# An encoder layer in fp32 halves: two gate products swapped, w_down's blocks in nine buffers, keys kept negated, and a split queued behind an addition

## The chip, the cores and the metric

The kernel runs on one core of a Trainium2 chip. The metric is the device time of one execution in microseconds; the time of a kernel is the median over its runs. The profile shows one execution of its own, taken by the hardware profiler. Engines are named as there: PE (matmul), PEld (its weight loader), DVE (vector engine), ACT (scalar engine), POOL (GpSimd), SP (the engine that issues most DMAs).

## The reference

One layer of a bidirectional encoder over 512 tokens of width 1024, all in float32, with 256 fixed memory tokens:

```python
memn = rms_norm(mem, mem_norm_g)
n = rms_norm(h, mix_norm_g)
proj = n @ w_in
gate_a, gate_b = sigmoid(proj[..., OFF_GA:OFF_GB]), sigmoid(proj[..., OFF_GB:])
ya = s5_branch(proj[..., :OFF_U], ...)          # state space, both directions
yb = sgu_branch(zu, zv, ...)                    # spatial gating in chunks of 128
h = h + (gate_a * (ya @ w_proj_a) + gate_b * (yb @ w_proj_b)) @ w_out
# memory cross-attention, 4 heads of 256
hn = rms_norm(h, xattn_norm_g)
q, k, v = hn @ w_q, memn @ w_k, memn @ w_v
s = einsum('blhd,bmhd->bhlm', q, k) * (256 ** -0.5)
h = h + einsum('bhlm,bmhd->blhd', softmax(s), v).reshape(...) @ w_xo
# SwiGLU, hidden width 2816
f = rms_norm(h, ffn_norm_g)
h = h + (silu(f @ w_gate) * (f @ w_up)) @ w_down
out = rms_norm(h, final_norm_g)
```

## The kernel before

**Precision.** Every matmul operand x is kept as two rounded halves, hi and lo, with x = hi + lo. `split` makes them: ACT casts x to hi (line 85), DVE subtracts hi from x to give lo (line 86). A product is three matmuls, hi·hi, hi·lo and lo·hi (`mm3`).

**Weights.** Weight blocks of 512 KB are loaded from DRAM by SP's queue into buffers tagged "raw" (three of them in the pool `wp`), split into "hi" and "lo" (three buffers each), and used by PE. A list `plan` holds one entry per block, in the order of use: a key, its loads with a number of entries by which each is asked for ahead, and a function `make` that splits the block. `next_w` hands out the blocks in that order: when entry i is used, it asks for the loads that are due (`LOADS` = 3 entries ahead unless the entry says otherwise) and for the splits of entries up to i + 2 (`SPLITS`).

**Seven products in place of eight.** Several large products (the gates of the second branch, the queries, gate and up projections, w_down) are done as 2 x 2 blocks with seven block products instead of eight, numbered 1, 5, 2, 6, 3, 7, 4. They need sums of weight blocks and of token blocks. For w_down, the sums of weights are made in DRAM: an SP copy into `dsum` (line 311), then a POOL DMA that adds the other block onto it (line 312), placed along the plan by `plan_sums`. The sums of tokens are made by DVE in place in `make_tokens`.

**Gates.** The two halves of the second gate (i = 0, 1) are interleaved by `ORDER`, whose entries are (product, half). Products 1, 6, 7 and 4 of a half accumulate in one bank gx[i], 5 and 3 in gq[i], 1 (copied) and 2 in gv[i]. After product 7, `kept` copies gx to SBUF on ACT (line 1250) and `minus` subtracts it from gq on DVE (line 1254). The weight of product 4 is made in place from product 6's: a DVE subtraction and then a POOL DMA that adds a block onto it (line 256).

**Attention.** `k_evac` splits the keys from PSUM into kt_hi and kt_lo. `scores` computes, for each head and each pair of token tiles, psc = q·k; then a row maximum `mx` (line 1528), its scaled negative `nm` (line 1529), two exponentials with `nm` as bias that also sum up (line 1531), a reciprocal and two scalings (line 1535). `turn_probs` transposes the probabilities on PE (line 1545).

**FFN.** `plan_units` and `plan_unit` make the gate and up projections in ten units; their blocks sit in "raw" and in two buffers each of the tags "b21", "t" and "b22" of a pool `stp[0]` that stays open to the end of the kernel. w_down follows: seven products of six blocks each (CHUNKS), from `plan_down`, the first two of them set between the last unit's products. For each product `make_tokens` splits the tokens for two blocks at a time (tag "s" in the profile). Results are added onto h by `onto_h` (line 1876), tile by tile. Near the end, products 7 and 4 use the same two banks dx[0] and dx[1] one after the other; `row_by_row` does two blocks for token tile 0 first and then for token tile 1.

**Order of the work.** Matmuls and other instructions are given in program order, but the order in each engine's queue is laid down ahead of time by a list scheduler that goes by priorities and its own costs (`schedule_with_timeline_sim=True`); on the chip each engine then works through its queue in that order, waiting on semaphores. `tc.issue_after(x)` puts the instructions traced in its block behind x, for those of them that run on x's engine; `keep_in_program_order` keeps one in its place.

Of the kernel before, what the change touches and what calls it, by code (L numbers as in the profile page):

```python
# [17 lines left out]
P = 128  # L18
# [34 lines left out]
def hybrid_layer_kernel(  # L53
# [29 lines left out]
    def split(dst_hi, dst_lo, src):  # L83

        hi = nc.scalar.copy(dst_hi, src)  # L85
        lo = nc.vector.tensor_tensor(dst_lo, src, dst_hi.bitcast(F32), ALU.subtract)  # L86
        if pinned[0]:
            in_order(hi)
            in_order(lo)
        return hi, lo  # L90
# [131 lines left out]
            plan.append(((w_q, 512 * n, q), [(LOADS, load)], lambda got=got: halves(got.pop("raw"))))  # L222

    GATES = [(w_in, OFF_GB), (w_in, OFF_GB + 512)]
    ORDER = ((1, 0), (1, 1), (2, 0), (2, 1), (5, 0), (6, 0), (5, 1), (7, 0), (6, 1), (3, 0), (7, 1), (4, 0), (4, 1), (3, 1))
    gate_place = [None]

    def plan_gates():
# [83 lines left out]
            plan[j + step][1].append((0, lambda d=dst, x=more: nc.gpsimd.dma_start(d, x, accum_op=ALU.add)))  # L312

    def plan_down(w, make_tokens, entries):
        for q in DOWN:
            for c in range(CHUNKS):
                got = {}

                def load(q=q, c=c, got=got):
                    src = down_block(*DSRC[q], c) if q in DSRC else down_sum(q, c)  # L320
                    got["raw"] = wp.tile([P, 2, 512], F32, tag="raw", name="wraw", bufs=3)[:, :src.shape[1]]
                    nc.sync.dma_start(got["raw"], src)

                def make(q=q, c=c, got=got):
                    make_tokens(q, c)
                    return halves(got.pop("raw"))

                entries.append(((w, q, c), [(LOADS, load)], make))

    plan_tok(w_in, OFF_V, KD)  # L330
    for c0 in range(0, SW, 256):
# [1128 lines left out]
    kt_lo = ap_.tile([P, KD, M], F32R, name="kt_lo")  # L1460
    vts = []

    def k_evac(m, j, ps):
        split(kt_hi[:, m, :], kt_lo[:, m, :], ps)

    def v_evac(half):
        def f(t, ps):
# [44 lines left out]

    def scores(hd, behind=None):
        q_hi, q_lo = qs.pop(hd)
        scale = XD ** -0.5
        prob = ap_.tile([P, NT, M], F32, tag="prob", name="prob", bufs=1) if hd % 2 == 0 else \
            np_.tile([P, NT, M], F32, tag="gain", name="prob", bufs=2)
        for i in range(2):
            ps = bank("psc").rearrange("p (t m) -> p t m", t=2)
            for tt in range(2):  # L1520
                t = 2 * i + tt
                tsl = slice(t * P, (t + 1) * P)
                for k in range(2):
                    with nullcontext() if behind is None else tc.issue_after(behind):
                        mm3(ps[:, tt, :], (q_hi[:, k, tsl], q_lo[:, k, tsl]),
                            (kt_hi[:, 2 * hd + k, :], kt_lo[:, 2 * hd + k, :]), k == 0, k == 1)
            mx, nm, sm, rs = (ap_.tile([P, 2], F32, tag=k, name=k, bufs=4) for k in ("mx", "nm", "sm", "rs"))
            nc.vector.tensor_reduce(mx, ps, AX.X, ALU.max)
            nc.vector.tensor_scalar(nm, mx, -scale, None, ALU.mult)
            for tt in range(2):  # L1530
                nc.scalar.activation(prob[:, 2 * i + tt, :], ps[:, tt, :], AF.Exp, bias=nm[:, tt:tt + 1],
                                     scale=scale, accum_out=sm[:, tt:tt + 1])
            nc.vector.reciprocal(rs, sm)
            for tt in range(2):
                nc.vector.tensor_scalar(prob[:, 2 * i + tt, :], prob[:, 2 * i + tt, :], rs[:, tt:tt + 1], None, ALU.mult)
        return prob
# [201 lines left out]

    made, last_job = {}, []

    def token_pieces(f, ts, c):
        if c < 2:
# [3 lines left out]
    def make_tokens(q, c):  # L1748

        if c % 2 or (q, c // 2) in made or (q, c) == (1, 0) and not last_job:  # L1750
            return
        c //= 2
        hi, lo = made[q, c] = sums_place((1, 2, 4)[len(made) % 3], 4, 256)
        f, ts = {1: (0, T0), 5: (0, T1), 6: (0, T1), 2: (1, T0), 7: (0, T0), 3: (1, T0), 4: (1, T1)}[q]
        for src, ks in token_pieces(f, ts, c):
            split(hi[:, ks], lo[:, ks], src)
        a, b_, c_, d_ = (token_pieces(f_, ts_, c) for ts_ in (T0, T1) for f_ in (0, 1))
        for (q11, _), (q12, _), (s21, _), (q22, _) in zip(a, b_, c_, d_):
            if q == 5:
                V.tensor_tensor(s21, s21, q11, ALU.subtract)  # L1760
            elif q == 3:
                V.scalar_tensor_tensor(q11, s21, -1.0, q22, ALU.mult, ALU.subtract)
            elif q == 2:
                V.tensor_tensor(q12, q12, s21, ALU.add)
# [108 lines left out]
    def onto_h(ps, t0, half, op):  # L1873
        for t in range(2):
            hs = h[:, t0 + t, HALF[half]]
            nc.vector.tensor_tensor(hs, hs, ps[t], op)  # L1876

    def row_by_row(q, c0):

# [21 lines left out]
        finish(t)  # L1901
    down_product(dx, 7, False, range(CHUNKS - 2))
    row_by_row(7, CHUNKS - 2)
    onto_h(dx, 2, 0, ALU.subtract)
    for t in range(2, 4):
        first_half(t, 0)

    held = []
    row_by_row(4, 0)
    for c in range(2, CHUNKS):  # L1910
        ops_ = next_w(w_down, 4, c)
        if c < CHUNKS - 2:
            rows_product(dx, 4, c, ops_, (0, 1), slice(0, 512), False, c == CHUNKS - 3)
        else:
            held.append((c, ops_))
# [46 lines left out]
```

## Time and profile before

| | |
|---|---|
| median of three runs | 869.28 us (869.12 to 870.82) |
| the profiled execution | 870.48 us, span 868.7 us |
| granted TensorE clock | 0.996 |
| busy PE, PEld, DVE, ACT, POOL | 855.1, 760.1, 648.3, 474.8, 106.0 us |
| instructions | 14845 |
| HBM read, written | 148.70 MB, 37.20 MB |

The span runs from the first to the last instruction of the program; the execution's own time has what lies around it. Times in rows of the trace are counted from the start of the span. The kernel's stages lie roughly so: gates from 262 to 303 us, attention's scores from 457 to 487, the units from 543 to 760, w_down from there to the end. In a row of the timeline stand start, duration, engine, line, operation, out<-in, shapes and count, and in brackets how long the engine had been idle and what released it.

### The profile page before, as it was taken

To read this page: it belongs to the slowest core of one execution; us is meant where nothing else is said; L and a number is where in the kernel's file an instruction comes from. 1 tells how busy PE (TensorE), PEld (TensorE's weight loads), DVE (VectorE), ACT (ScalarE), POOL (GpSimd) and SP (SyncE) were. 2 spreads that over 40 slices of the span, in tenths; PEclk is the share of its full clock that TensorE was granted. 3 is DMA by queue.
4 is the path that set the end of the run, shared out by engine and by line. 5 is a ranking of instruction groups with operands and counts; after the bars stand their busy time and mean duration, and the time that the engine had idled before them with its cause. 6 is when DMAs were issued, how large, how long until landed. Compare 5 with 4: busy or idle time off the path is not lost.

```text
span 868.7 us, 14845 instructions
## 1 busy us (share of the span) xinstructions
PE 855.1 (98%) x5894; PEld 760.1 (88%) x5894; DVE 648.3 (75%) x897; ACT 474.8 (55%) x704; POOL 106.0 (12%) x157
## 2 busy tenths in 40 slices
PE   8999999999999999999999999999999999999996
PEld 6788888888789988899899888999999999987875
DVE  5699589968748668679658646767877778898875
ACT  5544875276437534467457444655545454655664
POOL 1001155100601000110010001001111111000000
PEclk9999999999999999999999999999999999999999
DMA  7549279745639586944687143557798786476572
GB/s 247 163 115 265 66 216 242 160 128 169 158 92 252 138 230 206 274 124 160 217 257 214 53 151 103 146 146 178 166 240 230 183 222 143 134 213 216 201 246 94
DMA packets 110119, 155.40 MB, mean 179 GB/s; under 512 B 8969, under 2 KB 77089, under 8 KB 109986
## 3 DMA queue, kind: packets, MB, share of 16 engines
q1 hardware_dynamic: 91746, 128.27, 44.9%
q0 software_dynamic: 18016, 25.66, 18.5%
q8 instruction: 46, 0.75, 0.3%
q10 hardware_dynamic: 288, 0.52, 0.2%
q14 instruction: 23, 0.19, 0.1%
HBM read 148.70 MB, written 37.20 MB: 214 GB/s over the span
## 4 chain that ended last, share of the span: by engine, by line
PE 91%; DMA 3%; ACT 2%; DVE 2%; issue 1%; SPq 0%; POOL 0%; POOLq 0%; ACTq 0%; DVEq 0%
PE pf L396 25%; PE pt L396 18%; PE px L1241 13%; PE dx L396 7%; PE pq L1241 6%; PE pv L1241 3%; PE gx L1241 3%; PE qx L1241 3%; PE dq L396 2%; PE gq L1241 1%; PE psc L396 1%; PE po L396 1%; PE qq L1241 1%; PE py L1034 1%; PE ptr L563 1%
## 5 line engine op out<-in xcount | busy, mean ns | idle before, releaser
L85 ACT CAST whi<-wraw 128x1024 fp32r<-128x1024 f32 (+1 forms) x133 | 136.9, 1029 | 143.1 <-PE pf L396 42.1
L86 DVE TENSOR_TENSOR wlo<-wraw,whi 128x1024 fp32r<-128x1024 f32 (+1 forms) x133 | 158.5, 1192 | 71.9 <-ACT whi L85 70.9
L396 PE MATMUL pf<-xn,whi 128*128 128x512 f32 x320 | 99.8, 392 | 0.0
L1241 PE MATMUL px<-fn,whi 128*128 128x256 f32 x480 | 83.2, 276 | 0.0
L1241 PEld LDWEIGHTS px<-fn,whi 128*128 128x128 f32 x480 | 72.5, 188 | 0.2
L396 PEld LDWEIGHTS pf<-xn,whi 128*128 128x128 f32 x320 | 59.6, 188 | 12.5 <-issue 0.5
L85 ACT CAST whi<-b 128x1024 fp32r<-128x1024 f32 x40 | 42.2, 1054 | 51.4 <-PE px L1241 26.5
L86 DVE TENSOR_TENSOR wlo<-b,whi 128x1024 fp32r<-128x1024 f32 x40 | 48.9, 1222 | 28.5 <-ACT whi L85 28.5
L1241 PE MATMUL px<-fn,wlo 128*128 128x256 f32 x240 | 66.4, 277 | 0.0
L396 PE MATMUL pf<-xn,wlo 128*128 128x512 f32 x160 | 62.9, 393 | 0.0
L1241 PE MATMUL pq<-s,whi 128*128 128x256 f32 x320 | 55.0, 276 | 0.0
L396 PE MATMUL dx<-whi,s 128*128 128x512 f32 x170 | 53.3, 391 | 0.4 <-DVE h L1876 0.4
L86 DVE TENSOR_TENSOR wlo<-t,whi 128x1024 fp32r<-128x1024 f32 x30 | 36.7, 1224 | 19.4 <-ACT whi L85 19.4
L85 ACT CAST whi<-t 128x1024 fp32r<-128x1024 f32 x30 | 31.6, 1054 | 35.3 <-PE pv L1241 12.6
L1241 PEld LDWEIGHTS pq<-s,whi 128*128 128x128 f32 x320 | 48.2, 188 | 0.0
L1241 PEld LDWEIGHTS px<-fn,wlo 128*128 128x128 f32 x240 | 45.1, 188 | 0.0
L1241 PE MATMUL pq<-s,wlo 128*128 128x256 f32 x160 | 44.2, 276 | 0.0
L396 PE MATMUL pt<-whi,xn 128*128 128x512 f32 x128 | 42.8, 407 | 0.3 <-ACT xn L85 0.2
L396 PEld LDWEIGHTS dx<-whi,s 128*128 128x128 f32 x170 | 31.8, 188 | 7.6 <-issue 0.8
L312 POOL DMA_DIRECT2D dsum<-in_w_down_dram x12 | 13.3, 1108 | 189.8 <-DMA dsum<-in_w_down_dram 189.8
L396 PEld LDWEIGHTS pf<-xn,wlo 128*128 128x128 f32 x160 | 30.1, 188 | 6.3 <-issue 0.2
L396 PE MATMUL dx<-wlo,s 128*128 128x512 f32 x85 | 32.9, 389 | 0.0
(480 smaller groups left out, 2329.5 us busy)
## 6 DMA issues: line engine op xcount, KB each, us to landing
wraw<-in_w_in_dram SPq DMA_DIRECT2D x35, 512.0 KB, 5.8
dsum<-in_w_down_dram SPq DMA_DIRECT2D x20, 512.0 KB, 5.9
wraw<-dsum SPq DMA_DIRECT2D x20, 512.0 KB, 3.7
b<-in_w_gate_dram SPq DMA_DIRECT2D x15, 512.0 KB, 4.3
b<-in_w_up_dram SPq DMA_DIRECT2D x15, 512.0 KB, 5.2
wraw<-in_w_down_dram SPq DMA_DIRECT2D x15, 512.0 KB, 4.8
dsum<-in_w_down_dram POOLq DMA_DIRECT2D x10, 512.0 KB, 7.5
dsum<-dsum POOLq DMA_DIRECT2D x10, 512.0 KB, 6.4
```

The lines of the kernel that those rows point to most:

```text
L85: hi = nc.scalar.copy(dst_hi, src)
L86: lo = nc.vector.tensor_tensor(dst_lo, src, dst_hi.bitcast(F32), ALU.subtract)
L312: plan[j + step][1].append((0, lambda d=dst, x=more: nc.gpsimd.dma_start(d, x, accum_op=ALU.add)))
L396: last_mm[0] = nc.tensor.matmul(ps, a[x], b[y], start=start and i == 0, stop=stop and i == 2, skip_group_check=free)
L563: tr = nc.tensor.transpose(ps[:, j, :], src[:, k * P:(k + 1) * P], ident)
L1034: in_order(nc.tensor.matmul(ps[64 * j:64 * j + 64, :], a, b, start=g % 4 == k == 0, stop=k == 2, tile_position=(0, 64 * j), skip_group_che ...
L1241: nc.tensor.matmul(ps[:, j, :], a[x], b[y], start=start and j == k == i == 0, stop=k == 3 and i == 2, skip_group_check=True)
```

## The change

Four places are edited.

1. `ORDER` has (4, 0) where (3, 0) stood, and the reverse, two places apart with (7, 1) between them.
2. `plan_down` gives its blocks buffers in a fixed turn: three "raw", and two each of "b21", "t" and "b22", nine in all; every block from the third on asks for its load six entries ahead rather than three. The first two blocks stay as they were.
3. `k_evac` stores the keys times -1/16 (a scaled activation on ACT and a multiply-subtract on DVE). So psc comes out as minus the scaled scores; a row minimum of it is directly the bias, the exponential runs with scale -1, and the instruction that scaled and negated the maximum is gone.
4. `onto_h` returns its first addition. That of product 7 is kept in `held_back` until product 4's first two blocks have been taken, and `make_tokens` traces its splits behind it meanwhile.

```diff
-    ORDER = ((1, 0), (1, 1), (2, 0), (2, 1), (5, 0), (6, 0), (5, 1), (7, 0), (6, 1), (3, 0), (7, 1), (4, 0), (4, 1), (3, 1))
+    ORDER = ((1, 0), (1, 1), (2, 0), (2, 1), (5, 0), (6, 0), (5, 1), (7, 0), (6, 1), (4, 0), (7, 1), (3, 0), (4, 1), (3, 1))
...
     def plan_down(w, make_tokens, entries):
+        turns = ("raw", "b21", "raw", "t", "b22", "raw", "b21", "t", "b22")
...
-                def load(q=q, c=c, got=got):
+                def load(q=q, c=c, got=got, n=len(entries)):
                     src = down_block(*DSRC[q], c) if q in DSRC else down_sum(q, c)
-                    got["raw"] = wp.tile([P, 2, 512], F32, tag="raw", name="wraw", bufs=3)[:, :src.shape[1]]
+                    tag = turns[n % len(turns)] if n > 1 else "raw"
+                    got["raw"] = (wp if tag == "raw" else stp[0]).tile(
+                        [P, 2, 512], F32, tag=tag, name="wraw", bufs=3 if tag == "raw" else 2)[:, :src.shape[1]]
                     nc.sync.dma_start(got["raw"], src)
...
-                entries.append(((w, q, c), [(LOADS, load)], make))
+                entries.append(((w, q, c), [(LOADS if len(entries) < 2 else 6, load)], make))
...
+    scale = XD ** -0.5
+
     def k_evac(m, j, ps):
-        split(kt_hi[:, m, :], kt_lo[:, m, :], ps)
+        nc.scalar.activation(kt_hi[:, m, :], ps, AF.Copy, scale=-scale)
+        nc.vector.scalar_tensor_tensor(kt_lo[:, m, :], ps, -scale, kt_hi[:, m, :].bitcast(F32), ALU.mult, ALU.subtract)
...
-        scale = XD ** -0.5
...
-            mx, nm, sm, rs = (ap_.tile([P, 2], F32, tag=k, name=k, bufs=4) for k in ("mx", "nm", "sm", "rs"))
-            nc.vector.tensor_reduce(mx, ps, AX.X, ALU.max)
-            nc.vector.tensor_scalar(nm, mx, -scale, None, ALU.mult)
+            nm, sm, rs = (ap_.tile([P, 2], F32, tag=k, name=k, bufs=4) for k in ("nm", "sm", "rs"))
+            nc.vector.tensor_reduce(nm, ps, AX.X, ALU.min)
             for tt in range(2):
                 nc.scalar.activation(prob[:, 2 * i + tt, :], ps[:, tt, :], AF.Exp, bias=nm[:, tt:tt + 1],
-                                     scale=scale, accum_out=sm[:, tt:tt + 1])
+                                     scale=-1.0, accum_out=sm[:, tt:tt + 1])
...
-    made, last_job = {}, []
+    made, last_job, held_back = {}, [], [None]
...
         for src, ks in token_pieces(f, ts, c):
-            split(hi[:, ks], lo[:, ks], src)
+            with nullcontext() if held_back[0] is None else tc.issue_after(held_back[0]):
+                split(hi[:, ks], lo[:, ks], src)
...
     def onto_h(ps, t0, half, op):
         for t in range(2):
             hs = h[:, t0 + t, HALF[half]]
-            nc.vector.tensor_tensor(hs, hs, ps[t], op)
+            added = nc.vector.tensor_tensor(hs, hs, ps[t], op)
+            first = added.ins if t == 0 else first
+        return first
...
-    onto_h(dx, 2, 0, ALU.subtract)
+    held_back[0] = onto_h(dx, 2, 0, ALU.subtract)
     for t in range(2, 4):
         first_half(t, 0)

     held = []
     row_by_row(4, 0)
+    held_back[0] = None
```

## The prediction

> **What bounds the kernel now.** I read the page first (engine totals), then the waits of PE, then the timeline around each wait that lies behind the first changed line, because a change here is worth only what PE stops waiting for.
>
> ```profile
> PE 855.1 (98%) x5894; PEld 760.1 (88%) x5894; DVE 648.3 (75%) x897; ACT 474.8 (55%) x704; POOL 106.0 (12%) x157
> ...
> PE ppt L1545 <- DVE prob L1535: 1.1, 1, 1.1
> ...
> PE dv L396 <- DVE wlo L86: 0.5, 1, 0.5
> ...
> PE dx L396 <- DVE h L1876: 0.4, 1, 0.4
> PE gq L1241 <- DVE u L1254: 0.4, 1, 0.4
> ...
> PE dv L396 <- ACT whi L85: 0.3, 1, 0.3
> ```
>
> PE is busy 98% of the span, so the bound is TensorE's stream of matmuls, and the change neither adds nor removes a matmul. What can be won is idle time of PE. The five waits shown are those that stand behind the gates; they add to 2.7 us, and each edit of the change touches one of them. But the idle column understates a stall: a matmul's drawn end overlaps its successor. I therefore price each stall by start times: the step over the gap, less the ordinary step.
>
> **Edit 1, gate products.** PE and DVE at the third product on gq, then ACT and POOL before it:
>
> ```profile
> 288.11 0.28 PE L1241 MATMUL gx<-gse,wlo 128*128 128x256 f32 x1
> 288.80 0.39 PE L1241 MATMUL gq<-gsd,whi 128*128 128x256 f32 x1 [0.41 <-DVE u L1254]
> 289.02 0.28 PE L1241 MATMUL gq<-gse,whi 128*128 128x256 f32 x1
> 289.14 0.28 PE L1241 MATMUL gq<-gsd,wlo 128*128 128x256 f32 x1
> 288.06 0.68 DVE L1254 TENSOR_TENSOR u<-gq,u 128x512 f32<-128x512 f32 x1
> 282.75 1.05 ACT L85 CAST whi<-wraw 128x1024 fp32r<-128x1024 f32 x1 [0.96 <-ACT u L1341]
> 286.79 0.58 ACT L1250 COPY u<-gx 128x512 f32<-128x512 f32 x1
> 276.50 1.35 POOL L256 DMA_DIRECT2D gw<-in_w_in_dram  x1 [1.82 <-issue]
> DMA to landing us min/median/max: 4.5/6.1/6.7
> ```
>
> The ordinary step of a 256-column matmul is 0.11-0.12 (289.02 to 289.14). The step over the gap is 0.69, and the next is 0.22 instead of 0.11: the stall costs 0.58 + 0.11 = 0.69. Product (3,0) accumulates into gq[0], which `minus` of product (7,0) still reads until 288.74, with one product in between. With (4,0) in its place PE writes gx[0], whose last reader is the copy that ends at 287.37, before PE gets there at about 288.2; (3,0), two products later, finds gq[0] long free. What moves with (4,0): its split goes into the slot where (3,0)'s ran, at 282.75, and it must find the POOL accumulation landed, issued at 276.50, so about 282.6 by the median and 283.2 by the maximum. That is a tie with 282.75, but behind it cast (1.05) and subtraction need some 2.3, and PE arrives at 288.2: 2.6 us of cover even at the maximum. The tiles' ring of "ev" buffers and the raw buffers keep their counts; (3,0)'s raw buffer is freed two products (2 x 24 matmuls of 0.113, 5.4) later, so w_glu's second block is fetched that much later on SP, and it is used five products and one block after that. Bounds: gain 0 (the tie goes wrong) to 0.69; the value is 0.69, since the cover is wide.
>
> **Edit 2, keys kept negated, one instruction less per pair of tiles.** DVE, then PE:
>
> ```profile
> 474.10 0.68 DVE L1528 TENSOR_REDUCE mx<-psc 128x2 f32<-128x512 f32 x1
> ...
> 476.43 0.16 DVE L1529 TENSOR_SCALAR nm<-mx 128x2 f32<-128x2 f32 x1
> ...
> 478.90 0.15 DVE L1533 RECIPROCAL rs<-sm 128x2 f32<-128x2 f32 x1
> 479.34 0.69 DVE L1528 TENSOR_REDUCE mx<-psc 128x2 f32<-128x512 f32 x1 [0.28 <-PE psc L396]
> ...
> 480.01 0.61 DVE L1535 TENSOR_SCALAR prob<-prob,rs 128x256 f32<-128x256 f32 x2
> 479.02 0.28 PE L396 MATMUL psc<-kt_hi,qq 128*128 128x256 f32 x1
> 480.41 0.70 PE L1545 MATMUL ppt<-ident,prob 128*128 128x128 f32 x4 [1.11 <-DVE prob L1535]
> L85 ACT CAST kt_hi<-pf x8: 363/373/381, 387.5 to 407.9; 128x256 fp32r<-128x256 f32 x8
> L1531 ACT ACTIVATE prob<-psc,nm x16: 462/473/495, 460.1 to 486.8; 128x256 f32<-128x256 f32 x16
> ```
>
> The stall is 480.41 - 479.02 - 0.11 = 1.28. Its cause is the order of DVE's queue: head 1's probabilities (480.01) stand behind a row reduction of head 2, which itself waits for PE until 479.34. They stand so late because the chain has four hops on DVE and ACT, and between hops DVE takes longer work: the reduction ended at 474.78, yet `nm` ran at 476.43. Without `nm` the exponentials can start right behind the reduction, up to 1.65 earlier; the reciprocal at 478.90 would then be possible near 477.3 and both scalings before PE asks at 479.1. Bounds: at the low end nothing but `nm`'s own slot goes (at most its 0.16), at the high end the whole 1.28; below zero only if the new order puts a second reduction in front, another 0.69. I take 1.28, as 1.65 is over it. The eight evacuations of keys become a scaled activation: the cast takes 0.373, an activation of the same shape from PSUM 0.473, so at most 8 x 0.10 = 0.8 of ACT in a stage where it has slack (55% busy over the span, no wait of PE there); DVE's two-input instruction keeps its shape. Price on PE: 0.
>
> **Edit 3, w_down's blocks in nine buffers, six ahead.** The chain of waits gives the load, PE the stall; then the waits of PE's weight loader, and DVE and DMA by windows:
>
> ```profile
> 784.78 7.41 DMA wraw<-in_w_down_dram
> 792.29 1.05 ACT L85 CAST whi<-wraw 128x1024 fp32r<-128x1024 f32 x1 [3.02 <-DMA wraw<-in_w_down_dram]
> 792.72 0.39 PE L396 MATMUL dv<-whi,s 128*128 128x512 f32 x1
> 793.39 0.73 PE L396 MATMUL dv<-whi,s 128*128 128x512 f32 x2 [0.28 <-ACT whi L85]
> 794.65 0.50 PE L396 MATMUL dv<-wlo,s 128*128 128x512 f32 x1 [0.53 <-DVE wlo L86]
> 794.99 0.62 PE L396 MATMUL dv<-whi,s 128*128 128x512 f32 x2
> 795.45 0.40 PE L396 MATMUL dv<-wlo,s 128*128 128x512 f32 x1
> PEld dv L396 <- DVE wlo L86: 1.2, 2, 1.0
> PEld dv L396 <- ACT whi L85: 0.7, 1, 0.7
> 760.00:780.00 20.00, 20.00 (x91) 16.61 (x90) 19.45 (x24) 11.48 (x15) 0.81 (x1) 1.00 0.73 201
> 780.00:800.00 20.00, 19.19 (x83) 14.92 (x82) 15.77 (x19) 10.78 (x13) 0.81 (x1) 1.00 0.70 220
> ```
>
> The ordinary step of 512 columns is 0.23 (two from 794.99 to 795.45). So the stalls are 0.67 - 0.23 = 0.44, then 1.26 - 0.46 = 0.80, then 0.34 - 0.23 = 0.11 on restart: 1.36 after rounding of starts. The load was issued only at 784.78, when a third buffer fell free, and took 7.41, so ACT sat 3.02. With nine buffers block n reuses that of block n-9, split long before load n is asked for; a block is 12 matmuls, 2.7 us, so a load is asked for some 6 x 2.7 = 16 us ahead, more than twice 7.41. SP's queue gets no new entry, only earlier ones; they pass the copies of w_down's sums and the output rows, and hold neither back, for no load stands waiting for a buffer except the first ones. Those come in a burst as the last unit ends: five blocks of 512 KB at 220 GB/s take about 12 us (an estimate from the windows row); the first is asked for no later than now, the fifth is used five blocks later. Who is late next is DVE: 19.45 of 20 us busy between 760 and 780. But it idles 4.2 us in the next 20, waiting for just these loads, and gets that time back. Bounds: 0.56 (only the first stall and the restart go, since DVE is behind) to 1.36; I take 1.36.
>
> Row against rule: by PE's rows these two waits are 0.8, by the start times 1.36. The Trainium skill, "Perfetto Trace Analysis", section on the most contended engine, says that matmul busy time is the wrong measure and that LDWEIGHTS should be judged; the two PEld rows give 1.9. By that the term would be 1.9 rather than 1.36. I keep the start times, because a weight load that waits while matmuls are still queued costs nothing.
>
> **Edit 4, splits behind h's first addition.** DVE, then PE:
>
> ```profile
> 844.36 1.22 DVE L86 TENSOR_TENSOR s<-a_low,s 128x1024 fp32r<-128x1024 f32 x1
> 845.76 1.29 DVE L1876 TENSOR_TENSOR h<-h,dx 128x512 f32<-128x512 f32 x2 [0.18 <-PE dx L396]
> 845.78 0.39 PE L396 MATMUL dx<-whi,s 128*128 128x512 f32 x1
> 846.59 0.47 PE L396 MATMUL dx<-whi,s 128*128 128x512 f32 x1 [0.42 <-DVE h L1876]
> 846.90 0.39 PE L396 MATMUL dx<-wlo,s 128*128 128x512 f32 x1
> ```
>
> The stall is 0.81 - 0.23 = 0.58 and 0.08 on restart: 0.66. Product 4 writes dx[0], which h's first addition still reads. Only one split falls between setting and clearing `held_back`: that of tokens (4, 1), the one at 844.36. The row of 845.76 is a warning: DVE had been idle for 0.18 and waited for PE, so the split was not what delayed it. PE finished dx[0] late, although `row_by_row` is written so that row 0 ends nine matmuls (2.0 us) before row 1. If block (7,5) is ready earlier, as edit 3 makes it, PE's order can be the written one; dx[0] is then complete near 844, and the split at 844.36 would be in the way: there the edit pays. Behind the held split on DVE stand h's second addition and the low half of block (4,1), which PE wants 1.4 us into product 4. Bounds: 0.66 if PE's order follows; -0.56 if it doesn't and the split of 1.22 pushes that low half, less the 0.66. I take half the gain, 0.33, between the row (0) and the written order (0.66).
>
> **Sum.** 0.69 + 1.28 + 1.36 + 0.33 = 3.66 us. The profiled execution took 870.48 (span 868.7) and would take 866.82. The median of the three timed runs is 869.28, 1.2 below it; the stalls belong to the order of work, not to profiling, so the forecast is 869.28 - 3.66 = 865.6. This measurement can tell about 0.2% (1.74 us) from no change.
>
> **Rivals.**
> (B) Only loads and gates pay: 0.69 + 1.36 = 2.05, so 867.2. For it: the probabilities' stall comes from a queue's order, which is laid down ahead of time from the scheduler's own costs and can fall wrong again; the row of 845.76 speaks against edit 4. The change then does not do what two of its parts say.
> (C) A new wait of the removed ones' size in each changed stage: the gates' 0.69 stays, the rest is paid back, 868.6. For it: DVE at 97% between 760 and 780.
> (D) Slower: DVE becomes the bound of w_down. There are 42 blocks, and one 1.22 us token split that the new order puts before a low half stalls PE by as much when no cover is left. Once in each of the seven products is 7 x 1.22 = 8.5; less edits 1 and 2 (1.97) that is 875.8; three such waits give 1.7 slower, 871.0, and that is the point from which it counts. Against: DVE's 4.2 us of idling between 780 and 800, and 14.92 of 20 on the loader there.
> (E) The measure by weight loads: with 1.9 for edit 3 and the whole 0.66 for edit 4 the sum is 4.53, 864.75. [...]
>
> **Chances.** The forecast has 0.47 (A), E 0.05, B 0.22, C 0.15, D 0.11. A's own range is 865.2 to 866.4. The range from 864.9 to 868.8 holds A, B, most of C and leaves out D and part of E, under 2 in 10. Faster by over 0.2% (under 867.54): A, E and nearly all of B, 0.73. Same: C and the rest of B, 0.16. Slower: D, 0.11.
>
> **What would show it.** No idle of PE before gq, dv, ppt and dx in the waits; `whi` no more released by a DMA in the w_down stretch; h's first addition starting about 2 us before row 1 ends. Wrong for edit 2 if probabilities still stand behind a reduction; for edit 3 if dv still waits on wlo though its load landed early; for edit 4 if h's addition still waits for PE. The forecast fails as a whole if DVE's waits by PE grow in the last 120 us.

## The result and the profile after

The changed kernel takes 868.24 us (median of 22 runs, 866.75 to 870.54), the kernel before 870.31 us beside it (22 runs, 868.35 to 874.2). The ratio is 0.9975, 95% interval 0.9967 to 0.9984: 2.2 us faster, where 3.66 were forecast. Three runs of 1738 to 3044 us (one of the kernel before, one each of `two` and `three2` below) are left out of all ratios. A second series of the same kernel (run `after2` below) gave 0.9967 (0.9954 to 0.9981). The profiled span went from 868.7 to 866.4 us.

The edits are numbered here as in the prediction: 1 the gate products, 2 the keys, 3 w_down's buffers, 4 the held split. (The list of the change above has the keys third and the buffers second.)

Busy time of the engines in the changed kernel, then PE's waits in it, and last the first wait as it was in the kernel before (in total, times, longest, in us):

```profile
PE 854.6 (99%) x5894; PEld 760.9 (88%) x5894; DVE 646.5 (75%) x889; ACT 475.5 (55%) x704; POOL 107.0 (12%) x157
...
PE pf L399 <- ACT yb_hi L85: 1.7, 1, 1.7
...
PE dx L399 <- DVE h L1881: 0.4, 1, 0.4
PE pf L396 <- ACT yb_hi L85: 1.4, 1, 1.4
```

Of the five waits behind the gates that the prediction listed, four are gone. The one that edit 4 aimed at is there with the same 0.4. The wait for yb_hi (the high half of the second branch's result) lies ahead of all changed stages, 1.7 here and 1.4 in the kernel before; it comes back below.

**Gates.** PE at the place of the old stall:

```profile
288.05 0.28 PE L1244 MATMUL gx<-gse,wlo 128*128 128x256 f32 x1
288.16 0.39 PE L1244 MATMUL gx<-gse,whi 128*128 128x256 f32 x2
288.39 0.28 PE L1244 MATMUL gx<-gse,wlo 128*128 128x256 f32 x1
```

PE goes straight on into a product on gx with steps of 0.11, where it stood for 0.69.

**Heads.** DVE, then PE:

```profile
474.00 0.68 DVE L1533 TENSOR_REDUCE nm<-psc 128x2 f32<-128x512 f32 x1
474.60 1.22 DVE L86 TENSOR_TENSOR wlo<-wraw,whi 128x1024 fp32r<-128x1024 f32 x1
475.73 1.28 DVE L86 TENSOR_TENSOR qq<-u,qq 128x512 fp32r<-128x512 f32 x2
476.94 0.16 DVE L1537 RECIPROCAL rs<-sm 128x2 f32<-128x2 f32 x1
477.01 0.67 DVE L86 TENSOR_TENSOR ot_lo<-po,ot_hi 128x512 fp32r<-128x512 f32 x1
477.60 0.60 DVE L1539 TENSOR_SCALAR prob<-prob,rs 128x256 f32<-128x256 f32 x2
...
479.68 0.69 DVE L1533 TENSOR_REDUCE nm<-psc 128x2 f32<-128x512 f32 x1 [0.28 <-PE psc L399]
479.35 0.28 PE L399 MATMUL psc<-kt_hi,qq 128*128 128x256 f32 x1
479.48 0.60 PE L1549 MATMUL ppt<-ident,prob 128*128 128x128 f32 x4
```

The reciprocal runs at 476.94 instead of 478.90 and the scalings at 477.60 instead of 480.01, ahead of the reduction that waits for PE (479.68) and not behind it. The transposes find them ready 0.13 behind the last score.

**w_down.** ACT at the casts of two blocks of w_down, then the engines by windows (busy of PE, PEld, DVE, ACT, POOL; granted clock, share and GB/s of the DMA engines):

```profile
786.66 1.05 ACT L85 CAST whi<-wraw 128x1024 fp32r<-128x1024 f32 x1 [0.39 <-PE dv L399]
789.38 1.05 ACT L85 CAST whi<-wraw 128x1024 fp32r<-128x1024 f32 x1 [1.67 <-PE dv L399]
780.00:800.00 20.00, 20.00 (x90) 16.57 (x89) 18.05 (x21) 12.64 (x15) 0.00 (x0) 1.00 0.64 210
```

The casts now wait for PE to free a half's buffer, not for a load: in the view of the loads of these blocks from 760 to 830 us no one waits for them, where ACT waited 19.4 us in 13 waits before. PE has no idle time between 780 and 800, where it had 0.81; DVE is busy for 18.05 of these 20 us, 15.77 before. How this comes about is seen when each load is paired with the cast of its block: from the fourth block on, a load left 5.1 us ahead of its cast in the median before, and leaves 20.0 us ahead now. The prediction took it that a load would no longer stand waiting for a buffer. In SP's queue they still do (31.0 us in 15 waits for a low half from 760 to 800), but so far ahead that ACT never waits for them.

**h's first addition.** PE, then DVE:

```profile
842.90 0.39 PE L399 MATMUL dx<-whi,s 128*128 128x512 f32 x1
843.13 0.39 PE L399 MATMUL dx<-wlo,s 128*128 128x512 f32 x1
843.36 0.39 PE L399 MATMUL dx<-whi,s 128*128 128x512 f32 x1
844.16 0.47 PE L399 MATMUL dx<-whi,s 128*128 128x512 f32 x1 [0.42 <-DVE h L1881]
840.79 1.23 DVE L86 TENSOR_TENSOR wlo<-wraw,whi 128x1024 fp32r<-128x1024 f32 x1 [1.10 <-ACT whi L85]
843.33 0.69 DVE L1881 TENSOR_TENSOR h<-h,dx 128x512 f32<-128x512 f32 x1 [1.32 <-PE dx L399]
843.93 1.22 DVE L86 TENSOR_TENSOR s<-a_low,s 128x1024 fp32r<-128x1024 f32 x1
```

The split (843.93) is now behind the addition (843.33), as the edit says. DVE had been idle for 1.32 us and waited for PE. The matmuls of the two token rows still alternate to the end of product 7, so the last one on dx[0] is two matmuls from the end of the product, and the step of 0.80 (0.58 above the ordinary one, by starts before rounding) stays.

**Where the 2.35 us of the two profiled spans lie.** The table gives, for each profiled execution, the start of the first pt matmul, the stall at the last yb_hi (its step less the ordinary one), and three stretches between first matmuls: from gx to yg (gates), from the first psc to the first on fn (heads and the output projection), and from the first dx to the closing pcut (w_down). In the kernel before these stretches begin at 261.95, 445.09 and 746.09 us, the last two earlier than the rough stages named ahead of the prediction. Between the stretches the executions agree to 0.2 us; only the long stretch from the first pt to the stall varies more (0.75), and in the row with a star the clock fell for a while just behind the stall (granted 0.52 between 220 and 225 us).

| kernel | first pt | yb_hi stall | gates | heads | w_down |
|---|---|---|---|---|---|
| before | 9.33 | 1.51 | 41.05 | 94.50 | 113.54 |
| before2 | 9.33 | 1.00 | 41.06 | 94.48 | 113.70 |
| gates (edit 1) | 9.35 | 1.03 | 40.37 | 94.48 | 113.66 |
| scores (edit 2) | 8.88 | 0.90 | 41.05 | 93.52 | 113.70 |
| hop_back | 9.01 | 1.07 | 41.05 | 94.51 | 113.00 |
| held (edit 4) | 9.17 | 1.22 | 41.16 | 94.48 | 112.25 |
| three_six_ahead | 9.23 | 1.31 | 41.06 | 95.27 | 113.30 |
| two (edits 1, 2) | 9.37 | 1.15 | 40.37 | 93.46 | 113.35 |
| down (edit 3) | 9.78 | 1.74 | 41.15 | 94.48 | 112.02 |
| down2 | 11.12 | 2.37 | 41.06 | 94.48 | 111.96 |
| nine_three_ahead | 9.57 | 2.61 | 41.06 | 94.33 | 111.97 |
| three2 (edits 1 to 3) * | 8.88 | 2.86 | 40.37 | 93.46 | 111.96 |
| after | 9.54 | 1.87 | 40.37 | 93.53 | 112.12 |
| after2 | 11.12 | 0.79 | 40.37 | 93.54 | 112.10 |
| rows_held | 11.12 | 1.94 | 40.37 | 93.54 | 111.34 |
| rows_free | 9.15 | 0.95 | 40.37 | 93.53 | 111.36 |
| rows_free2 | 8.88 | 2.20 | 40.37 | 93.46 | 111.31 |
| down_bd | 8.88 | none | 41.06 | 94.53 | 112.01 |
| rows_free_bd | 11.12 | none | 40.37 | 93.48 | 111.33 |

Changed against before: gates -0.68, heads -0.97, w_down -1.42, the units +0.13, and +0.62 ahead of the gates, where the program was not changed: -2.32, the rest is rounding. The kernel `three` is left out of the table, for its profiled execution ran at a granted clock of 0.943.

### The profile page after: what moved, and what is told of

Its sections match the earlier page's. It is cut to its first block, busy times and chain, and to the rows that moved or that the text cites. A ratio compares the mean times of both kernels' runs of the same rounds, so it can differ in the third digit from the quotient of the medians.

```text
span 866.4 us, 14832 instructions
## 1 busy us (share of the span) xinstructions
PE 854.6 (99%) x5894; PEld 760.9 (88%) x5894; DVE 646.5 (75%) x889; ACT 475.5 (55%) x704; POOL 107.0 (12%) x157
## 4 chain that ended last, share of the span: by engine, by line
PE 94%; DMA 2%; ACT 2%; issue 1%; DVE 1%; SPq 0%; POOL 0%; POOLq 0%; ACTq 0%
PE pf L399 25%; PE pt L399 18%; PE px L1244 13%; PE dx L399 7%; PE pq L1244 6%; PE dq L399 3%; PE pv L1244 3%; PE gx L1244 3%; PE qx L1244 3%; PE dv L399 2%; PE psc L399 1%; PE po L399 1%; PE qq L1244 1%; PE gq L1244 1%; PE py L1037 1%; PE ptr L566 1%
## 5 line engine op out<-in xcount | busy, mean ns | idle before, releaser
L86 DVE TENSOR_TENSOR wlo<-t,whi 128x1024 fp32r<-128x1024 f32 x30 | 36.7, 1224 | 19.4 <-ACT whi L85 19.4
```

## Experiments

### One edit at a time

The kernels `gates`, `scores`, `down` and `held` are the kernel before with one of the four parts of the diff each. T, R and S stand for the theory and the rivals that an expectation names.

> Edit 1 alone (products (3,0) and (4,0) swapped). Theory T (each edit is worth the PE stall that it takes away): the wait of PE gq on DVE u goes, the stretch from the first gx matmul to the first matmul on yg shortens by 0.6 to 0.7 us, everything behind keeps its length; 0.7 us faster in all, ratio about 0.9992. Rival R (the 0.62 us that the changed kernel's profiled run lost ahead of the gates comes from the swap, for instance by other transfers): the first gx matmul lies 0.5 us or more later than in the kernel before, and nothing is won in all. If the loss ahead of the gates is only the spread from one execution to the next, the first gx matmul lies at 262.0 to 262.6 in all runs without any pattern.

Measured: 869.89 us against 869.94, ratio 0.9997 (0.9983 to 1.0011). The gq wait is gone, the gates' stretch is 0.68 shorter, the heads and w_down are within 0.12 of before, and the first gx matmul is where it was (261.97 against 261.95). T holds in the trace; the time alone could not tell 0.7 us.

> Edit 2 alone (keys kept as -1/16, row minimum, no scaling of the maximum). Theory T: the wait of PE ppt on DVE prob (1.28 us by start times) goes, and the stretch from the first psc matmul to the first use of ot shortens by 1.0 to 1.3 us; 1.0 to 1.3 us faster in all, ratio 0.9985 to 0.9989. Rival R: in the whole change the head's stretch was shorter because other work had moved, and alone the edit leaves a ppt wait: less than 0.4 us.

Measured: 868.76 us, ratio 0.9991 (0.9979 to 1.0003). The ppt wait is gone, the heads' stretch is 0.98 shorter. By the stretch that the expectation names, to the first use of ot, it is 1.05 (38.69 to 37.65): T, at its lower end. The interval of the time holds T and no change alike.

> Edit 3 alone (w_down's blocks in nine buffers, six ahead). Theory T: the waits of PE dv on whi and wlo go, the stretch from the first dv matmul to the end shortens by 1.3 to 1.5 us, the stall ahead of h's first addition (0.66) stays, since PE's order of the last matmuls of product 7 stays interleaved; 1.4 us faster, ratio about 0.9984. Rival D of the prediction (DVE bound): new waits on wlo, no gain or a loss.

Measured: 870.17 us, ratio 1.0004 (0.9992 to 1.0015). In the trace both dv waits are gone and w_down is 1.52 shorter than in the kernel before, yet the time did not follow: T is right on the stretch and wrong on the time. This is the result that asked for the later runs.

> Edit 4 alone (token splits of the last blocks queued behind h's first addition). Theory T: the addition waits for PE's last matmul on dx[0], not for the split, so the stall of 0.66 us stays or grows by the split's place: 0.0 to +0.3 us, ratio 1.0000 to 1.0004. Rival R (the split was what delayed h's addition): 0.5 to 0.66 us faster, the wait of PE dx on DVE h gone.

Measured: 869.64 us, ratio 0.9997 (0.9982 to 1.0011). PE's waits of this kernel:

```profile
PE ppt L1545 <- DVE prob L1535: 1.1, 1, 1.1
...
PE dx L396 <- DVE h L1877: 0.4, 1, 0.4
PE gq L1241 <- DVE u L1254: 0.4, 1, 0.4
```

The wait for h is unchanged, its step is 0.58 over the ordinary one, as in the kernel before. So edit 4 does nothing: T. But the list shows something else: the waits on dv are missing although w_down's loads are the old ones. ACT at the block that was late in the kernel before:

```profile
791.15 1.05 ACT L85 CAST whi<-wraw 128x1024 fp32r<-128x1024 f32 x1 [2.75 <-DMA wraw<-in_w_down_dram]
```

The load was issued at 784.55 and the cast began 6.6 us later; in the kernel before it was 784.78 and 7.5. That was enough: w_down took 112.25, not 113.54. The stall that edit 3 removes depends on transfers, and this execution did without it. It is the exception: the other seven executions with three buffers in the table took 113.00 to 113.70.

### Is it the row order of PE? And does edit 4 help then?

`three` is the change without edit 4. `rows_held` is the whole change, and `rows_free` is `three`, both with this edit, which makes PE finish the first token row of the last two blocks before it begins the second:

```diff
-    def row_by_row(q, c0):
+    def row_by_row(q, c0, strict=False):
...
         for t in range(2):
-            for c, ops_ in pair_:
-                rows_product(dx, q, c, ops_, (t,), slice(0, 512), False, c == CHUNKS - 1)
+            with tc.issue_after(last_mm[0].ins) if strict and t == 1 else nullcontext():
+                for c, ops_ in pair_:
+                    rows_product(dx, q, c, ops_, (t,), slice(0, 512), False, c == CHUNKS - 1)
...
-    row_by_row(7, CHUNKS - 2)
+    row_by_row(7, CHUNKS - 2, True)
```

> The whole change without edit 4. Theory T (edit 4 is worth nothing, because h's first addition waits for PE): the same time as the whole change, ratio to the kernel before about 0.9965 to 0.9975, and PE's wait for DVE h of 0.4 us is there as in the whole change. Rival R (edit 4 pays): 0.3 to 0.66 us slower than the whole change.

Measured: 867.68 us against 870.34, ratio 0.998 (0.9957 to 1.0002); the changed kernel beside it (`after2`) 867.75. No difference.

> The whole change, and in product 7 the matmuls of the second row tile of the last two blocks are queued behind the last matmul of the first row tile, so that PE finishes dx[0] some 2 us before dx[1]. Theory T (the order of PE's last matmuls is what keeps the 0.66 us stall): h's first addition starts about 2 us ahead of row 1's end, PE's wait for DVE h goes, 0.5 to 0.66 us faster than the whole change, ratio to the kernel before 0.001 below that of the whole change. Rival R (something else, DVE's load of work, sets it): the addition is earlier, and another wait of 0.4 us or more appears at block (4,0) or (4,1).

Measured: 867.43 us, ratio 0.9965 (0.9953 to 0.9977). PE's wait for h is gone, and w_down is 0.76 shorter than in `after2`: T in the trace. The time is only 0.3 under `after2`, which these runs can't tell from nothing.

> Edits 1 to 3 with the same strict order of rows on PE, but no splits held back. If edit 4 is of use once PE's order is right: the 1.22 us split stands in front of h's first addition and the stall is larger than with held splits by up to 0.6 us. If the scheduler places h's addition by itself, as soon as PE's order makes it ready early: same time as with the held splits within 0.2 us, and edit 4 is not needed in either case.

Measured: 866.46 us (6 runs), ratio 0.9952 (0.9933 to 0.9971). DVE of `rows_free` at the end of product 7, and PE:

```profile
839.88 1.23 DVE L86 TENSOR_TENSOR wlo<-wraw,whi 128x1024 fp32r<-128x1024 f32 x1 [1.11 <-ACT whi L85]
841.03 0.68 DVE L1880 TENSOR_TENSOR h<-h,dx 128x512 f32<-128x512 f32 x1
841.62 1.22 DVE L86 TENSOR_TENSOR s<-a_low,s 128x1024 fp32r<-128x1024 f32 x1
842.45 0.61 PE L399 MATMUL dx<-whi,s 128*128 128x512 f32 x2
842.90 0.39 PE L399 MATMUL dx<-wlo,s 128*128 128x512 f32 x1
```

The addition (841.03) runs right behind the low half before it, with no idle time, and ahead of the split (841.62), though nothing holds the split back; PE goes on without a gap. Both kernels with the strict order have the same w_down, 111.34 and 111.36. What the edit of the change wanted is had by PE's order alone, and worth 0.65 to 0.76 us of w_down in the traces.

> The changed kernel once more. Ratio to the kernel before 0.9967 to 0.9984 as measured. Its first gx matmul was at 262.56 us in the profiled run, against 261.95 in the kernel before, with the same order of instructions on every engine ahead of it: if that is the spread between executions, it lies anywhere from 261.9 to 262.6 here; if it belongs to the changed kernel, at 262.5 again.

Measured: 867.75 us, ratio 0.9967 (0.9954 to 0.9981). The first gx matmul is at 263.27, later still, because the first pt matmul is at 11.12 instead of 9.5, while the yb_hi stall is at its least, 0.79. So neither number belongs to the changed kernel as such; the expectation had the range too narrow.

### Hops, buffers, distance

`hop_back` is edit 2 with a copy put back, which gives the chain its old number of instructions on DVE:

```diff
-            nc.vector.tensor_reduce(nm, ps, AX.X, ALU.min)
+            mn_ = ap_.tile([P, 2], F32, tag="mx", name="mx", bufs=4)
+            nc.vector.tensor_reduce(mn_, ps, AX.X, ALU.min)
+            nc.vector.tensor_scalar(nm, mn_, 1.0, None, ALU.mult)
```

> Edit 2, with one instruction put back that does nothing but cost a place in VectorE's queue: the row minimum is copied (times 1.0) before the exponentials use it. Theory T (the stall of ppt comes from the number of hops in the chain and from the order of VectorE's queue that follows): the wait of PE ppt on DVE prob is back with its 1.28 us by start times, the stretch from the first psc matmul to the first use of ot is 38.6 to 38.8 us as in the kernel before, where edit 2 has 37.6. Rival R (scaled keys, or the minimum in place of the maximum, make the difference): 37.6 to 37.8 us, no ppt wait.

Measured: 870.05 us against 869.61, ratio 1.0003 (0.9988 to 1.0017). DVE and PE:

```profile
475.82 0.16 DVE L1532 TENSOR_SCALAR nm<-mx 128x2 f32<-128x2 f32 x1
...
478.71 0.69 DVE L1531 TENSOR_REDUCE mx<-psc 128x2 f32<-128x512 f32 x1 [0.27 <-PE psc L396]
479.32 0.16 DVE L1532 TENSOR_SCALAR nm<-mx 128x2 f32<-128x2 f32 x1
479.39 0.61 DVE L1538 TENSOR_SCALAR prob<-prob,rs 128x256 f32<-128x256 f32 x2
478.40 0.28 PE L396 MATMUL psc<-kt_hi,qq 128*128 128x256 f32 x1
479.79 0.70 PE L1548 MATMUL ppt<-ident,prob 128*128 128x128 f32 x4 [1.11 <-DVE prob L1538]
```

The keys are scaled and the row minimum is used, and the stall is back to the hundredth (1.11, 1.28 by start times), with the scalings behind the waiting reduction again. One instruction of 0.16 us decided a stall of 1.28: by its place in the queue, not by its length.

`nine_three_ahead` is edit 3 with the old distance of three entries, `three_six_ahead` the old three buffers with a distance of six:

```diff
-                entries.append(((w, q, c), [(LOADS, load)], make))
+                entries.append(((w, q, c), [(LOADS if len(entries) < 2 else 6, load)], make))
```

> Edit 3 with its nine buffers, but the loads asked for three blocks ahead as in the kernel before. Theory T (the block that was late waited for a free buffer, then took 6.5 to 7.4 us): the load is now asked for earlier than 784 us and the dv stall is gone or under 0.3 us, since three blocks of 2.7 us are more than 7.4; gain 1.2 to 1.4 us in the stretch from the first dv matmul to the end against an execution of the kernel before with the stall. Rival R (the distance does it, not the buffers): the stall of 0.7 to 1.36 us stays.

Measured: 869.37 us, ratio 0.9995 (0.9981 to 1.0009). No wait on dv, w_down 111.97, as short as with six ahead. The loads leave 20.0 us ahead of their casts, as in the whole change: it is the nine buffers that let them go, and the distance adds nothing.

> Loads of w_down asked for six blocks ahead, but into the three buffers as before. Theory T (buffers hold the load back): the loads wait in SyncE's queue for a buffer, so the late one is issued at the same place relative to PE as before and the stall is 0 to 1.36 us like that of the kernel before, or worse, as other transfers stand behind the waiting load in that queue. Rival R (distance is enough): no dv stall.

Measured: 870.53 us, ratio 1.0014 (1.0001 to 1.0028), slower. PE's waits:

```profile
PE ppt L1545 <- DVE prob L1535: 1.4, 2, 1.1
...
PE dv L396 <- DVE wlo L86: 0.5, 1, 0.5
```

The late low half is still there (w_down 113.30), one block earlier than in the kernel before, behind a load that took 8.1 us. The loads leave 5.1 us ahead of their casts as before, and between 770 and 800 us they stand in SP's queue for 22.2 us until a low half is made and a buffer free (21.9 before). So the buffers held the loads back. The new distance also changed the order laid down for the heads: a second wait on the probabilities came, and that stretch is 0.77 longer.

> The kernel before once more, for the spread from one execution to the next. The stalls set by the order of a queue (0.58 at gq, 1.28 at ppt, 0.58 at h's addition) are there again with the same size within 0.02 us. The stall of dv, which hangs on how long one transfer takes, is anything from 0 (transfer under 6.5 us) to 1.4 us. The first pt matmul starts at 8.9 to 11.1 us and the stall ahead of the pf matmuls on yb_hi is 0.8 to 1.9 us, whatever the kernel.

Measured: 870.73 us, ratio to the other runs of the same kernel 1.0004 (0.9989 to 1.002). The stalls that a queue's order sets came back at 0.58, 1.28 and 0.58; w_down took 113.70, with the stall of dv at 1.63 by start times, above the range expected.

### Where edit 3's gain went

In the table the three-buffer kernels have a yb_hi stall of 0.90 to 1.51, 1.15 on average of eight; the ten with nine buffers that keep the old place of the zeroing (`three` with its 1.59 is one) have 0.79 to 2.86, 1.89 on average. In `down`, every engine's instructions ahead of that place are those of the kernel before, in the same order. Four more runs: `two` (edits 1 and 2), `three2`, `down2` and `rows_free2`, repeats of `three`, `down` and `rows_free`.

> Edits 1 and 2 without edit 3. From the stretches of the single edits: 0.68 (first gx to first yg) and 1.04 (first psc to first use of ot), 0.1 lost behind the heads; 1.6 us faster than before, ratio 0.9981. From the first dx to the first pcut at the end it should take what the kernel before takes, 112.3 to 113.7 us by the length of one transfer. Theory T (edit 3 is worth about 1.5 us in most executions): 1.2 to 1.5 us slower than the kernel with edits 1 to 3. Rival R (edit 3 is worth about 0.4 us as the timed runs of it alone suggest, since in most executions the late transfer comes in time): within 0.6 us of it, and dx to pcut nearer 112.3.

Measured: 869.0 us against 870.27, ratio 0.9977 (0.9967 to 0.9988; the quotient of the two medians is 0.9985); w_down 113.35.

> Edits 1 to 3 once more, beside the kernel without edit 3. Theory T: 1.2 to 1.5 us faster than edits 1 and 2 alone, dx to pcut 112.0 to 112.2. Rival S (edit 3 costs something ahead of w_down): the stall at the last yb_hi, far ahead of the change, is 1.5 us or more again, where kernels with three buffers had 0.9 to 1.5.

Measured: 868.38 us, ratio 0.9979 (0.9967 to 0.999); w_down 111.96, yb_hi stall 2.86. With edit 3, w_down is 1.4 shorter than in `two`, the stall 1.7 longer in the profiled execution, and the times don't differ by what they can tell. So the stretch is as T says and the time as R says, but not for R's reason, since the stall in w_down was there; S came.

> Edit 3 alone once more. Theory T: the second series gives 0.9985, the first one's 1.0004 was the spread of executions. Rival R: about 0.9995 again. Rival S as above: the stall at the last yb_hi is 1.5 us or more again; if it is 0.8 to 1.3 us, the stall is the spread of one transfer, whatever the kernel.

Measured: 868.85 us, ratio 0.9985 (0.9974 to 0.9996), with a yb_hi stall of 2.37. Edit 3 alone has now given 1.0004 and 0.9985; the two intervals overlap, near 0.9994.

> The best version so far, edits 1 to 3 with the strict order of rows and no held splits, beside edits 1 to 3 alone. By the stretch from dx to pcut it should be 0.75 us faster than these (111.35 against 112.1); ratio to the kernel before 0.9955 to 0.9965.

Measured: 866.77 us, ratio 0.9955 (0.9943 to 0.9968), w_down 111.31, against 111.96 in `three2`.

How that stall comes about is seen in `three2`: the chain of waits, POOL, then ACT.

```profile
207.52 9.18 DMA gw<-in_w_in_dram
217.29 1.30 POOL L262 DMA_DIRECT2D gw<-in_w_in_dram  x1 [19.33 <-DMA gw<-in_w_in_dram]
218.63 0.57 POOL L862 MEMSET bd<- 128x256 f32 x2
218.98 0.60 ACT L865 COPY bd<-bbr 64x128 f32<-64x128 f32 x2 [5.30 <-POOL bd L862]
219.59 0.60 ACT L865 COPY bd<-bbi 64x128 f32<-64x128 f32 x2
220.22 0.62 ACT L85 CAST yb_hi<-zu 128x512 fp32r<-128x512 f32 x1
```

POOL waits to issue an accumulating transfer until a block of the gates has landed, 9.18 us after its issue. The zeroing of `bd` is next in POOL's queue, ACT's copies into `bd` wait for it, and the cast of yb_hi that PE needs is behind the copies in ACT's queue. It needs none of what it waits for. This holds in every one of the eighteen executions that have the stall (those of the table and `three`): the stall is the block's landing time less 6.33 us, to within 0.03. `down_bd` and `rows_free_bd` move the last zeroing to DVE:

```diff
-            nc.gpsimd.memset(t, 0.0)
+            (nc.vector if o == 3 else nc.gpsimd).memset(t, 0.0)
```

> Edit 3 alone, with one zeroing (bd of the last group) moved from GpSimd to VectorE. On GpSimd it stood behind an accumulating transfer that waits for a block of the gates to land (7 to 9.2 us after its issue), and ScalarE's copies into bd and the last cast of yb_hi stood behind it; here the cast comes ahead of the copies. Theory S (the nine-buffer kernels lose 0.7 us on average at that stall): the stall at the last yb_hi is gone or under 0.2 us, so edit 3's 1.5 us in w_down and the stall of the kernel before (0.9 to 1.5 us) both show in the time: 2.0 to 2.7 us faster, ratio 0.997 to 0.9977. Rival: the wait returns at the next matmuls on bd (pk), and the gain is 0.5 to 1.5 us as with edit 3 alone.

Measured: 867.86 us against 870.32, ratio 0.9977 (0.9967 to 0.9987), with the stall gone and w_down 112.01. That is edit 3 alone, where it had given 1.0004 and 0.9985. But this gain (2.0 us by the ratio, 2.5 by the medians) holds two things, for the kernel before has the stall as well: taking off its average of 1.15 leaves 0.9 to 1.3 for edit 3, by estimate.

> The best version so far (edits 1 to 3, strict order of rows, no held splits) with the same zeroing moved from GpSimd to VectorE: the stall at the last yb_hi (0.95 and 2.20 us in its two profiles) gone, 1.0 to 2.0 us faster than without, ratio to the kernel before 0.9935 to 0.995. Rival: the wait returns at pk, ratio 0.9953 as before.

Measured: 865.52 us (5 runs), ratio 0.9944 (0.9927 to 0.9962): 4.8 us faster than before, more than the changed kernel, and the lowest median of all, though its interval overlaps that of `rows_free`. ACT:

```profile
218.41 0.62 ACT L85 CAST yb_hi<-zu 128x512 fp32r<-128x512 f32 x1 [2.39 <-DVE zu L1222]
219.82 0.60 ACT L865 COPY bd<-bbr 64x128 f32<-64x128 f32 x2 [0.79 <-DVE bd L862]
```

The cast goes ahead of the copies and follows the values that it casts. Behind the first 26 us PE has no wait of over 0.15 us left in this kernel.

What stays open: why the block of the gates lands later in the kernels with nine buffers. That it does is fairly clear, for the two kernels with the moved zeroing have the transfer too: eight executions with three buffers took 7.2 to 7.9 us (7.5 on average), twelve with nine buffers 7.1 to 9.2 (8.2), ten of them no less than the longest of the eight. The order of instructions ahead of the place is the same. The kernel before with the zeroing moved was not run.

## Why the prediction was right or wrong

The direction and the mechanisms of edits 1 to 3 held; the forecast of 865.6 is 2.6 us under the measured 868.24. About 1.0 of this is the base, 1.6 the edits. Of the sum of 3.66 the two profiled executions show 2.32. Missing are 0.33 of edit 4, 0.31 of edit 2, 0.13 in the units and 0.62 ahead of the gates; edit 3's stretch gave 0.06 more than its term. So two terms were wrong, and the step from PE's stalls to the time, which takes it that nothing else moves, was wrong too.

**Base.** 3.66 was taken off a median of three runs, 869.28. Over the 16 to 35 runs of each later comparison the same kernel's median is 869.61 to 870.34. The prediction saw that its profiled execution was 1.2 above that median, and put this aside because the stalls belong to the order of work. Some of the spread does not: the first pt matmul starts anywhere from 8.88 to 11.12 us, the yb_hi stall is from 0.79 to 2.86, and w_down's from 0 to 1.6.

**Edit 1, 0.69:** right, 0.68 in every execution with the swap. The tie that could have gone wrong, 2.6 us of cover, did not show.

**Edit 2, 1.28:** right in cause, since `hop_back` reproduces it, too large in size. The stall went as a whole, but the stretch is only 0.97 shorter (0.96 to 1.04 in the kernels with the edit). The other 0.3 is in the steps around: the 32 transposing matmuls take 3.19 us between starts in `scores` and 2.94 in `hop_back`, those of the queries 0.2 more, and the output projection 0.2 less. A sum of stalls by start times counts how long PE stood, not what the new order costs. The scaled evacuation cost PE nothing, as priced.

**Edit 3, 1.36:** the mechanism is right, and its size too in the stretch: 1.42 against the profile of before. Of the two measures that the prediction set against each other, the start times (1.36) agree with it, and the 1.9 of the waiting weight loads does not. The Trainium skill, "Perfetto Trace Analysis", section on the most contended engine, judges by weight loads how close a kernel is to roofline; it does not say that a single stall is to be priced by them, so these runs don't speak against it. `nine_three_ahead` and `three_six_ahead` show which half of the edit works: the buffers. What failed is the step from this stall to the time. The size was no luck of one execution: w_down took 113.3 on average of the eight executions with three buffers, 112.0 of the seven with nine and the old order of rows, 1.3 less; only against `held` (112.25) was there 0.2 to win. But the prediction listed only the waits behind the first changed line. The wait ahead of them, 1.4 in the same list, was left out as untouched; in the kernels with nine buffers it was 0.74 longer on average. That leaves some 0.6 us of the 1.3, and edit 3 alone was 0.9985 to 1.0004 of the time before. With that wait removed (`down_bd`) the time follows the stretch, as far as the estimate there goes. Why edit 3 goes with a later landing is open.

**Edit 4, 0.33:** this is the step that failed outright. The row of 845.76, with DVE idle and waiting for PE, was read rightly as a sign that the split delayed nothing. The prediction then gave half the gain back on the thought that PE's order would be the written one once block (7,5) came early. PE's order is laid down ahead of time; in the changed kernel no cast of w_down waited for a load and the order stayed interleaved. `held` and `three` put the edit at nothing, `rows_free` shows that the order of PE's rows is the whole of it. The loss that was feared, 0.56, did not come either: w_down took 112.10 and 112.12 with the edit, 111.96 to 112.02 without.

**Rivals.** B, with gates and loads alone (2.05 off the median, 867.2), came nearest in the size of the gain, but by chance, since edit 2 did pay. C, at 868.6, lies nearest the measured time, but only because the base was 1.0 too low: no new wait of PE came in a changed stage. The time of A, 865.6, and that of E, 864.75, are both too low. D, with DVE as the bound of w_down, fell: DVE is 18.05 of 20 us busy between 780 and 800 and PE has no idle time there. Of the signs announced, PE's idle time ahead of gq, ppt and dv went, but not that ahead of dx. No cast was released by a load any more. H's first addition 2 us ahead of row 1's end came only in the kernels with the strict order of rows. The sign against edit 4, h's addition still waiting for PE, came. So did the sign that was to fail the whole forecast: in the last 120 us DVE waited 5.0 us for PE, 3.5 before. It was a poor sign, for w_down became shorter all the same, and 1.1 of the 1.5 is DVE idle ahead of h's first addition (1.32, 0.18 before).

## What to carry to other kernels

A short instruction in a chain is worth its place in the queues that it passes, not its length; look for what stands ahead of the work that somebody waits for, as with the copy of 0.16 us that brought a stall of 1.28. When the consumer waits for the producer's last matmul, holding other work back from the consumer is useless: change the producer's order. Price a stall that hangs on a transfer by several executions (here w_down was 0.2 to 1.7 us longer in eight of them). And read the waits that the change doesn't touch too: a gain that is whole in its own stretch need not reach the time, when a stall elsewhere grows with it.

## What the runs showed of the hardware

The same transfer, issued at the same point of PE's stream (within 0.2 us, counted from the first py matmul), landed after quite different times: 7.86 us in the kernel before, 7.10 in `after2`, and 9.18 in `three2` (its line stands above).

```profile
207.67 7.86 DMA gw<-in_w_in_dram
209.79 7.10 DMA gw<-in_w_in_dram
```

Four of the profiled executions, of four different kernels, have their first pt matmul at 11.12 us to the hundredth; the others lie between 8.88 and 9.78. This was not followed up.
